# One product over three rows in place of two: the level updates of a gated scan

## The chip, the core and the metric

The kernel runs on one core of a Trainium2 chip. The metric is the device time of one execution in microseconds; a kernel's time is the median of its runs. TensorE (PE) multiplies matrices, VectorE (DVE) and ScalarE (ACT) work on elements, GpSimd (POOL) does small things and issues some DMAs, SyncE (SP) issues the others. Each engine has its own instruction stream and takes it in order; semaphores tie the streams together.

## The reference

One step of a decoder layer: RMS norm, a projection of 2048 prompt tokens and 8 decode tokens from 1024 to 8 × 512 columns, two groups of four heads of width 128, a head norm, a SiLU gate, the output projection, the residual and a final norm. The first four heads are retention with a fixed decay; the other four, HGRN2, have a decay of their own for each token and key column, and the change lies in these:

```
logf = logaddexp(log(lb), log1p(-lb) + log_sigmoid(hf))     # f = lb + (1 - lb) sigmoid(hf)
kin  = (1 - lb) * sigmoid(-hf)
q    = silu(hq)
S_t  = diag(f_t) S_{t-1} + k_t v_t^T,   o_t = S_t^T q_t       # computed in chunks
```

Inside a chunk the scores are A[t, s] = sum over d of q[t, d] k[s, d] times the product of f[., d] from s+1 to t. It is this product of decays that the levels build up.

## The kernel before, in words

Before about 570 us the kernel makes the projections of values, gates and the retention group, and runs the retention heads. Then come the HGRN2 heads, eight **units**: four heads for the first 1024 tokens, then the same four for the second 1024. A unit's keys and queries lie as [128 key columns, 1024 tokens] and its chunks have 128 tokens. At the end stands the output projection (lines 1648 to 1899).

The work on a unit is spread over three iterations. In the first, PE makes its f and q projections (matmuls of line 1039), each as three products of high and low parts. ACT turns them into f (line 1088) and k (line 1089), DVE into q and qt = q f (lines 1096 and 1098). In the second iteration the scan's **levels** run (`hgrn_rec`). In the third comes the **rest** (`tail_steps`, line 1106): the states (lines 1126 to 1134), the outputs (lines 1142 and 1144; the latter reads qt), their squares on ACT (line 1148), a reciprocal root on POOL (lines 111 and 112), the gated norm on DVE (line 1157), a transpose on PE (line 1164), an ACT copy (line 1166) and a store. So three units are in work at a time: while one is projected, the one before is scanned, and the one before that is finished.

The levels have block sizes b = 1, 2, 4, ... 64 (line 31). At each, small PE matmuls make the scores between the left and the right half of every block of 2b tokens, and then k of the left halves is multiplied by the decay over the right half, and qt of the right halves by the decay over the left half. That is `update` (lines 1220 to 1230): two DVE products of 512 columns each, lines 1225 (k) and 1228 (qt). The decays of all blocks come from `products` (line 1216). A unit has seven updates.

Three times in a unit (levels 1, 3 and 5) `keep` (line 1232) copies k and the right halves of qt to a buffer with two ACT instructions (lines 1235, 1236) before it updates them. The kept copy feeds the matmuls of one level (line 1255, or 1300 at level 5), the updated tiles those of the next (line 1255, or 1305 at level 6). So a pair of matmul groups can run while the next update is being made. `put` (line 1261) merges a level's scores on DVE under a mask.

What sets the order: PE's instructions stand as the program writes them. `merge` puts the steps of the levels and of the rest among the projection matmuls at written fractions of the iteration (the lists at the end of `hgrn_rec`). The order on the other engines is made by the framework's scheduler from its own estimates, except where `behind` (line 124) puts a step behind the last instruction issued on DVE, ACT and SP. Buffers come from pools: f, k and the pair q, qt have two buffers each, so a new unit's tile can be written when the tile of two units before is no longer read. Other work shares DVE and ACT in these iterations: the splits of weights and inputs into high and low parts (lines 115, 116), the output weights' sums (lines 1358 to 1364), and the decode tokens (lines 855 to 874).

Of the kernel before, what the change touches and what calls it, by code (L numbers as in the profile page):

```python
# [10 lines left out]
F32 = mybir.dt.float32  # L11
# [3 lines left out]
ALU = mybir.AluOpType  # L15
# [3 lines left out]
P = 128  # L19
# [3 lines left out]
HALF = T // 2  # L23
NB = 8
# [17 lines left out]
def step_kernel(ctx, tc, a, out):  # L42
    nc = tc.nc
    pe, act, dve, pool, sp = nc.tensor, nc.scalar, nc.vector, nc.gpsimd, nc.sync
# [960 lines left out]
    pools = {}  # L1005
# [48 lines left out]
    def sub_steps(half, j, name, evac, seg_list=None):  # L1054
        box = []

        def w():
            if not box:
                box.append(w_next(j))
            return box[0]  # L1060

        return [seg_steps(w, half, seg, name, evac) for seg in SEGS[half]]
# [6 lines left out]
    def hgrn_proj(half, h):  # L1069
        name = f"h{half}{h}"  # L1070
        u = {}

        def alloc():
            if not u:
                for x, b in (("f", 2), ("k", 2)):
                    u[x] = pools["ep"].tile([P, HALF + NB], F32, tag=f"u{x}", name=f"{x}{name}", bufs=b)
                u["qq"] = pools["ep"].tile([P, 2, HALF + NB], F32, tag="uqq", name=f"qq{name}", bufs=2)
                u["q"], u["qt"] = u["qq"][:, 0], u["qq"][:, 1, :HALF]
            return u

        def evac_f(t0, n, ps):
            f, k = alloc()["f"], u["k"]
            tt = slice(t0, t0 + n)
            xr = pools["tp"].tile([P, 512], F32, tag="tmp", name=f"fx{name}{t0}")
            sg = pools["tp"].tile([P, 512], F32, tag="tmp", name=f"fs{name}{t0}")
            act.activation(sg[:, :n], ps, AF.Sigmoid)
            act.activation(xr[:, :n], ps, AF.Sigmoid, scale=-1.0)
            act.activation(f[:, tt], sg[:, :n], AF.Identity, scale=lb1[:, h : h + 1], bias=lb[:, h : h + 1])
            act.activation(k[:, tt], xr[:, :n], AF.Copy, scale=lb1[:, h : h + 1])

        def evac_q(t0, n, ps):
            f, q, qt = (alloc()[x] for x in ("f", "q", "qt"))
            tt = slice(t0, t0 + n)
            sg = pools["tp"].tile([P, 512], F32, tag="tmp", name=f"qs{name}{t0}")
            act.activation(sg[:, :n], ps, AF.Sigmoid)
            dve.tensor_tensor(q[:, tt], ps, sg[:, :n], op=ALU.mult)
            m = min(t0 + n, HALF)
            dve.tensor_tensor(qt[:, t0:m], q[:, t0:m], f[:, t0:m], op=ALU.mult)

        steps = [  # L1100
            sub_steps(half, HF * NH + h, "f" + name, evac_f),
            sub_steps(half, HQ * NH + h, "q" + name, evac_q),
        ]
        return u, steps
# [83 lines left out]
    def hgrn_rec(half, h, u):  # L1188
        name = f"h{half}{h}"
        hd = NH + h  # L1190
        f, k, q, qt = u["f"], u["k"], u["q"], u["qt"]
# [8 lines left out]
        def views(b):  # L1200
            return (
                qt.rearrange("p (n two b) -> p n two b", two=2, b=b),
                k[:, :HALF].rearrange("p (n two b) -> p n two b", two=2, b=b),
            )

        def spans(li):
            if li == 0:
                return f[:, :HALF]
            at = HALF - (HALF >> (li - 1))
            return box["fp"][:, at : at + (HALF >> li)]  # L1210
# [8 lines left out]

        def update(li):  # L1220
            b = LEVELS[li]
            qv, kv = views(b)
            nb = HALF // (2 * b)
            two = spans(li).rearrange("p (n two) -> p n two", two=2)
            dve.tensor_tensor(  # L1225
                kv[:, :, 0, :], kv[:, :, 0, :], two[:, :, 1:2].to_broadcast([P, nb, b]), op=ALU.mult
            )
            dve.tensor_tensor(  # L1228
                qv[:, :, 1, :], qv[:, :, 1, :], two[:, :, 0:1].to_broadcast([P, nb, b]), op=ALU.mult
            )  # L1230

        def keep(li):
            b = LEVELS[li]
            ss = pools["ep"].tile([P, 3 * 512], F32, tag="kept", name=f"kept{name}{li}")
            act.activation(ss[:, 512:], k[:, :HALF], AF.Copy)  # L1235
            act.activation(
                ss[:, :512].rearrange("p (n b) -> p n b", b=b), views(b)[0][:, :, 1, :], AF.Copy
            )
            box["kept"] = ss
            update(li)  # L1240
# [26 lines left out]
        def scores0():  # L1267
            box["Ab"] = pools["up"].tile([P, CH, 32], F32, tag="Ab", name=f"Ab{name}")
            pa = ps_lv.tile([P, CH, 2, 32], F32, tag="lv", name=f"pa{name}")
            for c in range(CH):  # L1270
                for i in range(4):
                    cc = slice(c * P + 32 * i, c * P + 32 * i + 32)
                    pe.matmul(pa[32 * i : 32 * i + 32, c], k[:, cc], u["qq"][:, :, cc], start=True, stop=True)
            update(0)
            dve.tensor_tensor(
                box["Ab"], pa[:, :, 0], id32.unsqueeze(1).to_broadcast([P, CH, 32]), op=ALU.mult
            )
            put(pa[:, :, 1].rearrange("p c (n two b) -> p c n two b", two=2, b=1)[:, :, :, 1, :], 0)
            keep(1)

        def level(li, n):
            b = LEVELS[li + n]
            if n == 0:
                box["pl"] = ps_lv.tile([P, 2, CH, 16], F32, tag="lv", name=f"pl{name}{li}")
                small(box["pl"][:, 0], li, box["kept"])
            else:
                small(box["pl"][:, 1], li + 1)
                update(li + 1)
            put(box["pl"][:, n].rearrange("p c (n b) -> p c n b", b=b), li + n)
            if n:  # L1290
                keep(li + 2)
# [185 lines left out]
    def unit(i):  # L1477
        half, h = order[i]
        u, subs = hgrn_proj(half, h)
        steps = []  # L1480
        if i in SEG_MAJOR:
            for n in range(len(SEGS[half])):
                group = []
                for sub in subs:
                    group += sub[n]
                if (i, n) in sides:
                    group = weave(group, sides[i, n](), 0.0, 1.0 if i not in (3, 7) or (i, n) == (3, 1) else 0.6)
                steps += group
        else:
            for sub in subs:  # L1490
                for g in sub:
                    steps += g
        return steps, u
# [73 lines left out]
    for i in range(len(order)):  # L1567
        fill, u = unit(i)
# [297 lines left out]
    op = ctx.enter_context(tc.tile_pool(name="op", bufs=1))  # L1866
# [117 lines left out]
```

## Time and profile before

| | |
|---|---|
| runs | 1041.09, 1041.21, 1044.4 us; median 1041.21 |
| the profiled execution's span | 1040.8 us |
| busy: PE, DVE, ACT, POOL | 1028.0, 746.6, 554.1, 125.8 us |
| products of line 1225 / 1228 | 56 each; 0.69 / 0.68 us |
| ACT copies of lines 1235 / 1236 | 24 each; 1.06 / 0.64 us |
| place of the updates in the span | 605 to 886 us |

A row of a timeline is: start, duration, engine, line, operation, the written tile, the read tiles, the shape, and in brackets how long the engine stood idle before it and what released it. A row of a group has the count behind x, the busy time in all and the mean, then the idle time before. In a row of busy time by stretch the figures stand in the order PE, PE's weight loads, DVE, ACT, POOL, granted clock, share of the DMA engines, GB/s. Names in tiles: `kh` is k, `qqh` the pair q and qt, `fh` the decays, `fph` their products, `kepth` the kept copy, `plh` and `pah` the scores' banks, `poh` the outputs, `obh` the normed outputs, `poth` their transposes.

### The profile page before, as it was taken

Reading aid. Unit: us, or ns where it says so; the run is one execution under the profiler, and the core shown is the slowest. Engines: PE = TensorE matmul, PEld = TensorE weight load, DVE = VectorE, ACT = ScalarE, POOL = GpSimd, SP = SyncE. Lnnn points to the kernel's source line nnn. Section 1 sums busy time; section 2 is a strip of 40 time slices with the busy share of each in tenths; the row PEclk is TensorE's granted clock in tenths of the full one; section 3 lists DMA queues with packets and bytes.
Section 4 is the critical chain, followed back from the end, with each engine's and each line's share of the span. In section 5 each row is a group of like instructions: output and inputs, shape, how many; then the busy total and the mean of one; then the engine's idle time right before and its main releaser. Section 6 shows DMA issues by size and latency. Waiting matters only on the chain.

```text
span 1040.8 us, 21338 instructions
## 1 busy us (share of the span) xinstructions
PE 1028.0 (99%) x8231; PEld 851.5 (82%) x8231; DVE 746.6 (72%) x1387; ACT 554.1 (53%) x1209; POOL 125.8 (12%) x231
## 2 busy tenths in 40 slices
PE   9999999999999999999999999999999999999997
PEld 7778778787778888888888889898878888888775
DVE  6886676888665876666665767868767676667886
ACT  7853345635435765545554756565555465533242
POOL 0210001000000111111111100111022112312122
PEclk9999999999999999999999999999999999999999
DMA  8689999679998975487775696754785195575652
GB/s 298 214 325 336 321 335 310 266 252 318 312 333 301 366 248 161 163 274 218 231 255 165 244 321 212 259 161 161 236 255 189 36 382 206 161 286 187 240 183 102
DMA packets 151270, 255.61 MB, mean 246 GB/s; under 512 B 11424, under 2 KB 79280, under 8 KB 151040
## 3 DMA queue, kind: packets, MB, share of 16 engines
q1 hardware_dynamic: 143584, 229.22, 65.2%
q0 software_dynamic: 7440, 24.76, 6.2%
q8 instruction: 65, 1.06, 0.4%
q14 instruction: 37, 0.30, 0.1%
q10 hardware_dynamic: 144, 0.26, 0.1%
HBM read 166.51 MB, written 87.69 MB: 244 GB/s over the span
## 4 chain that ended last, share of the span: by engine, by line
PE 87%; DMA 6%; ACT 3%; DVE 2%; issue 1%; SPq 1%; POOL 0%; POOLq 0%; ACTq 0%; DVEq 0%
PE po L360 11%; PE pjqh L1039 9%; PE pjfh L1039 9%; PE py L1662 4%; PE plh L1255 2%; DMA xn<-in_x_prompt 2%; PE poh L1142 1%; PE par L744 1%; PE puh L1126 1%; PE pur L751 1%; PE por L757 1%; DMA T3l<-ws1T 1%; PE poh L1144 1%; PE por L759 1%; PE pv20a L360 1%
## 5 line engine op out<-in xcount | busy, mean ns | idle before, releaser
L1039 PE MATMUL pjfh<-xh,w_h 128*128 128x512 f32 (+2 forms) x160 | 59.9, 375 | 0.0
L1039 PE MATMUL pjqh<-xh,w_h 128*128 128x512 f32 (+2 forms) x160 | 59.8, 374 | 0.0
L1235 ACT ACTIVATE kepth<-kh 128x1024 f32<-128x1024 f32 x24 | 25.4, 1060 | 62.8 <-DVE kh L1225 62.7
L1039 PE MATMUL pjqh<-xh,w_l 128*128 128x512 f32 (+2 forms) x160 | 55.8, 349 | 0.0
L1039 PE MATMUL pjfh<-xl,w_h 128*128 128x512 f32 (+2 forms) x160 | 55.7, 348 | 0.0
L1039 PE MATMUL pjfh<-xh,w_l 128*128 128x512 f32 (+2 forms) x160 | 55.7, 348 | 0.0
L1039 PE MATMUL pjqh<-xl,w_h 128*128 128x512 f32 (+2 forms) x160 | 55.7, 348 | 0.0
L1225 DVE TENSOR_TENSOR kh<-kh,fph 128x512 f32<-128x512 f32 x48 | 33.4, 696 | 25.2 <-PE plh L1255 15.0
L116 DVE TENSOR_TENSOR ab_l<-xr,ab_h 128x512 fp32r<-128x512 f32 (+1 forms) x40 | 37.3, 954 | 6.6 <-ACT ab_h L115 6.6
L782 DVE SCALAR_TENSOR_TENSOR obr<-por,omr,rg 128x128 f32<-128x128 f32 x64 | 18.0, 345 | 32.3 <-POOL omr L774 27.6
L115 ACT ACTIVATE ab_h<-xr 128x512 fp32r<-128x512 f32 (+1 forms) x40 | 32.4, 840 | 15.2 <-DVE xr L313 15.2
L772 ACT ACTIVATE obr<-por 128x128 f32<-128x128 f32 x64 | 16.8, 277 | 43.4 <-PE por L759 41.1
L419 ACT ACTIVATE vo<-vo 128x512 f32<-128x512 f32 x32 | 20.1, 629 | 27.3 <-DVE vo L413 13.7
L1039 PEld LDWEIGHTS pjqh<-xh,w_h 128*128 128x128 f32 x160 | 30.2, 188 | 5.1 <-issue 1.6
L1039 PEld LDWEIGHTS pjqh<-xh,w_l 128*128 128x128 f32 x160 | 30.1, 188 | 4.1
L1039 PEld LDWEIGHTS pjfh<-xh,w_l 128*128 128x128 f32 x160 | 30.1, 188 | 4.1
L1039 PEld LDWEIGHTS pjfh<-xh,w_h 128*128 128x128 f32 x160 | 30.2, 189 | 3.8
L1228 DVE TENSOR_TENSOR qqh<-qqh,fph 128x512 f32<-128x512 f32 x48 | 32.8, 683 | 0.0
L313 DVE SCALAR_TENSOR_TENSOR xr<-xr,g_in,rb 128x256 f32<-128x256 f32 x64 | 27.0, 480 | 7.8 <-issue 5.0
L1039 PEld LDWEIGHTS pjqh<-xl,w_h 128*128 128x128 f32 x160 | 30.2, 189 | 2.7
L1039 PEld LDWEIGHTS pjfh<-xl,w_h 128*128 128x128 f32 x160 | 30.3, 189 | 2.7
L1157 DVE SCALAR_TENSOR_TENSOR obh<-poh,orsh,v 128x128 f32<-128x128 f32 x64 | 18.0, 344 | 13.4 <-POOL orsh L112 13.4
(1840 smaller groups left out, 3385.6 us busy)
## 6 DMA issues: line engine op xcount, KB each, us to landing
xr<-a_dram SPq DMA_DIRECT2D x24, 512.0 KB, 5.5
S<-s_dram SPq DMA_DIRECT2D x24, 512.0 KB, 5.6
xn<-in_x_prompt SPq DMA_DIRECT2D x32, 256.0 KB, 3.6
xr<-in_x_t SPq DMA_DIRECT2D x16, 512.0 KB, 6.1
a_dram<-xr SPq DMA_DIRECT2D x16, 512.0 KB, 4.1
s_dram<-S SPq DMA_DIRECT2D x16, 512.0 KB
wgr<-in_w SPq DMA_DIRECT2D x16, 512.0 KB, 8.7
xr<-a_dram SPq DMA_DIRECT2D x32, 256.0 KB, 4.4
```

What stands on the lines that cost most here:

```text
L115: act.activation(h, src, AF.Copy)
L116: dve.tensor_tensor(l, src, h.bitcast(F32), op=ALU.subtract)
L313: dve.scalar_tensor_tensor(r[:, k], r[:, k], g_in[:, kk : kk + 1], spread_to[i], op0=ALU.mult, op1=ALU.mult)
L360: pe.matmul(ps, xx, ww, start=(first and n == 0), stop=(last and n == 2), skip_group_check=more)
L419: act.activation(o, src, AF.Silu)
L782: dve.scalar_tensor_tensor(o[:, cc], po[:, h], ms[:, h : h + 1], rb_of[c, "g"][:, cc], op0=ALU.mult, op1=ALU.mult)
L1039: pe.matmul(ps, ww[:, kk], x[:, k, b0 : b0 + n], start=(k == 0 and i == 0), stop=(k == KT - 1 and i == 2),)
L1225: dve.tensor_tensor(kv[:, :, 0, :], kv[:, :, 0, :], two[:, :, 1:2].to_broadcast([P, nb, b]), op=ALU.mult)
L1228: dve.tensor_tensor(qv[:, :, 1, :], qv[:, :, 1, :], two[:, :, 0:1].to_broadcast([P, nb, b]), op=ALU.mult)
L1235: act.activation(ss[:, 512:], k[:, :HALF], AF.Copy)
L1255: pe.matmul(dst[32 * i : 32 * i + 32, c], kk, qq, start=True, stop=True)
L1662: pe.matmul(ps, o[:, kk], w[:, k % 4, i * 512 : (i + 1) * 512], start=(k == 0 and n == 0), stop=(k == KT - 1 and n == 2),)
```

## The change

The tile k and the tile with the two rows q and qt become one tile `qk` with the rows q, qt, k, with two buffers as before. `update` becomes one DVE product of 1024 columns: its operand has a dimension of two, row qt from column b on and row k from column 0 on, which lie row − b columns apart; its other operand is the span of decays, left one for qt and right one for k. The number of columns multiplied is the same. Line numbers behind the place are lower by 4 in the kernel after.

```diff
         def alloc():
             if not u:
-                for x, b in (("f", 2), ("k", 2)):
-                    u[x] = pools["ep"].tile([P, HALF + NB], F32, tag=f"u{x}", name=f"{x}{name}", bufs=b)
-                u["qq"] = pools["ep"].tile([P, 2, HALF + NB], F32, tag="uqq", name=f"qq{name}", bufs=2)
-                u["q"], u["qt"] = u["qq"][:, 0], u["qq"][:, 1, :HALF]
+                u["f"] = pools["ep"].tile([P, HALF + NB], F32, tag="uf", name=f"f{name}", bufs=2)
+                u["qk"] = pools["ep"].tile([P, 3, HALF + NB], F32, tag="uqk", name=f"qk{name}", bufs=2)
+                u["qq"] = u["qk"][:, 0:2]
+                u["q"], u["qt"], u["k"] = u["qk"][:, 0], u["qk"][:, 1, :HALF], u["qk"][:, 2]
             return u
...
         def update(li):
             b = LEVELS[li]
-            qv, kv = views(b)
-            nb = HALF // (2 * b)
-            two = spans(li).rearrange("p (n two) -> p n two", two=2)
-            dve.tensor_tensor(
-                kv[:, :, 0, :], kv[:, :, 0, :], two[:, :, 1:2].to_broadcast([P, nb, b]), op=ALU.mult
-            )
-            dve.tensor_tensor(
-                qv[:, :, 1, :], qv[:, :, 1, :], two[:, :, 0:1].to_broadcast([P, nb, b]), op=ALU.mult
-            )
+            nb, row = HALF // (2 * b), HALF + NB
+            x = u["qk"][:, 1]
+            both = bass.AP(x.tensor, x.offset + b, [list(x.ap[0]), [row - b, 2], [2 * b, nb], [1, b]])
+            two = spans(li).rearrange("p (n two) -> p two n", two=2)
+            dve.tensor_tensor(both, both, two.unsqueeze(3).to_broadcast([P, 2, nb, b]), op=ALU.mult)
```

PE's and POOL's instructions keep their order. On DVE and ACT the scheduler makes a new one. Three places follow.

DVE, the first two updates of the first unit's scan, before:

```order
609 L1225 TENSOR_TENSOR kh_5675<-kh_5675,fh_5674 128x512
610 L1228 TENSOR_TENSOR qqh_5676<-qqh_5676,fh_5674 128x512
611 L1275 TENSOR_TENSOR Abh_5861<-pah_5862,pk 128x256
612 L1261 COPY_PREDICATED Abh_5861<-lmask,pah_5862 128x128
613 L1225 TENSOR_TENSOR kh_5675<-kh_5675,fph_5836 128x256x2
614 L1228 TENSOR_TENSOR qqh_5676<-qqh_5676,fph_5836 128x256x2
```

and in the kernel after:

```order
609 L1226 TENSOR_TENSOR qkh_5675<-qkh_5675,fh_5674 128x2x512
610 L1271 TENSOR_TENSOR Abh_5860<-pah_5861,pk 128x256
611 L1257 COPY_PREDICATED Abh_5860<-lmask,pah_5861 128x128
612 L1226 TENSOR_TENSOR qkh_5675<-qkh_5675,fph_5835 128x2x256x2
613 L1257 COPY_PREDICATED Abh_5860<-lmask,plh_5934 128x64x2
```

Each pair of rows has become one row; nothing else moved here.

ACT, where the second unit is scanned, the third projected and the first finished, before:

```order
520 L1088 ACTIVATE fh_6408<-fsh_6486,lb,lb_168 128x256
521 L1089 ACTIVATE kh_6409<-fxh_6485,lb_168 128x256
522 L1235 ACTIVATE kepth_6533<-kh_5923 128x1024
523 L1236 ACTIVATE kepth_6533<-qqh_5924 128x512
...
527 L1148 ACTIVATE jkh_6572,omsh_6565<-poh_6557 128x128
528 L1086 ACTIVATE fsh_6611<-pjfh_768_6491 128x264
529 L1087 ACTIVATE fxh_6610<-pjfh_768_6491 128x264
530 L1088 ACTIVATE fh_6408<-fsh_6611,lb,lb_168 128x264
531 L1089 ACTIVATE kh_6409<-fxh_6610,lb_168 128x264
532 L1148 ACTIVATE jkh_6599,omsh_6598<-poh_6589 128x128
533 L1148 ACTIVATE jkh_6601,omsh_6598<-poh_6589 128x128
```

and after:

```order
519 L1088 ACTIVATE fh_6397<-fsh_6474,lb,lb_168 128x256
520 L1231 ACTIVATE kepth_6520<-qkh_5920 128x1024
521 L1232 ACTIVATE kepth_6520<-qkh_5920 128x512
...
525 L1148 ACTIVATE jkh_6558,omsh_6551<-poh_6543 128x128
526 L1086 ACTIVATE fsh_6597<-pjfh_768_6479 128x264
527 L1087 ACTIVATE fxh_6596<-pjfh_768_6479 128x264
528 L1088 ACTIVATE fh_6397<-fsh_6597,lb,lb_168 128x264
529 L1089 ACTIVATE qkh_6398<-fxh_6399,lb_168 128x512
530 L1089 ACTIVATE qkh_6398<-fxh_6473,lb_168 128x256
531 L1148 ACTIVATE jkh_6585,omsh_6584<-poh_6575 128x128
532 L1089 ACTIVATE qkh_6398<-fxh_6596,lb_168 128x264
533 L1148 ACTIVATE jkh_6587,omsh_6584<-poh_6575 128x128
```

The three evacuations of k (line 1089) stood behind their own f; two of them have moved behind the first four squares (line 1148) and one in between the second four. In the later iterations one or two of them move in the same way.

DVE, the fourth unit's scan (the fifth is projected, the third finished), before:

```order
767 L116 TENSOR_TENSOR xl_7451<-xr_7581,xh_7450 128x1024
768 L1225 TENSOR_TENSOR kh_6971<-kh_6971,fph_7440 128x128x4
769 L1228 TENSOR_TENSOR qqh_6972<-qqh_6972,fph_7440 128x128x4
...
773 L1358 TENSOR_TENSOR wot_7611<-wot_7610,wot_7609 128x512
774 L1096 TENSOR_TENSOR qqh_7586<-pjqh_0_7593,qsh_7734 128x512
775 L116 TENSOR_TENSOR xl_7451<-xr_7616,xh_7450 128x1024
776 L1360 TENSOR_TENSOR wot_7609<-wot_7609 128x512
777 L1098 TENSOR_TENSOR qqh_7586<-qqh_7586,fh_7584 128x512
778 L1362 TENSOR_TENSOR wot_7611<-wot_7610,wot_7609 128x512
779 L1157 SCALAR_TENSOR_TENSOR obh_7746<-poh_7683,orsh_7700,v_7089 128x128 x4
```

and after:

```order
747 L1226 TENSOR_TENSOR qkh_6952<-qkh_6952,fph_7415 128x2x128x4
...
750 L1354 TENSOR_TENSOR wot_7583<-wot_7582,wot_7581 128x512
751 L1096 TENSOR_TENSOR qkh_7558<-pjqh_0_7565,qsh_7704 128x512
752 L116 TENSOR_TENSOR xl_7426<-xr_7588,xh_7425 128x1024
753 L1356 TENSOR_TENSOR wot_7581<-wot_7581 128x512
754 L116 TENSOR_TENSOR xl_7426<-xr_7554,xh_7425 128x1024
755 L1098 TENSOR_TENSOR qkh_7558<-qkh_7558,fh_7557 128x512
756 L1358 TENSOR_TENSOR wot_7583<-wot_7582,wot_7581 128x512
757 L1157 SCALAR_TENSOR_TENSOR obh_7716<-poh_7653,orsh_7670,v_7067 128x128 x4
```

One subtraction of 1024 columns (line 116) has moved from ahead of the update with b = 4 to between line 1096 and line 1157, where now two of them stand.

## The prediction

> **What bounds the kernel now.** I read the page's head first, then busy time by stretch for the part in which the change works, then the waits of TensorE (PE), then the rows around the moved instructions.
>
> ```profile
> span 1040.8 us, 21338 instructions
> PE 1028.0 (99%) x8231; PEld 851.5 (82%) x8231; DVE 746.6 (72%) x1387; ACT 554.1 (53%) x1209; POOL 125.8 (12%) x231
> ...
> PE 87%; DMA 6%; ACT 3%; DVE 2%; issue 1%; SPq 1%; POOL 0%; POOLq 0%; ACTq 0%; DVEq 0%
> ...
> L1225 DVE TENSOR_TENSOR kh<-kh,fph x48: 681/693/727, 607.6 to 885.0; 128x512 f32<-128x512 f32 x48
> ...
> 600.00:650.00 50.00, 50.00 (x836) 44.73 (x836) 36.78 (x81) 30.20 (x61) 0.20 (x2) 1.00 0.77 267
> ...
> sum 300.00, PE 300.00 PEld 253.64 DVE 217.78 ACT 172.95 POOL 38.70; mean PE 50.00 PEld 42.27 DVE 36.30 ACT 28.83 POOL 6.45
> ```
>
> PE is the bound, and the chain that ended last runs mostly through it. The updates run from about 605 to 886 us; in the six stretches of 50 us from 600 to 900 PE is busy for all 300.00 us, and the granted clock is 1.00 in the first of them (the column after POOL). VectorE (DVE) is busy for 217.78 of these 300 us, ScalarE (ACT) for 172.95. Busy PE need not be PE at its peak, so I looked at the list of its waits and at the pitch of its long matmuls (start, duration):
>
> ```profile
> PE pgd L600 <- DMA wgr<-in_w: 1.2, 2, 0.7
> ...
> 725.38 0.39 PE L1039 MATMUL pjfh<-xl,w_h 128*128 128x512 f32 x1
> ...
> 727.68 0.39 PE L1039 MATMUL pjfh<-xh,w_l 128*128 128x512 f32 x1
> 727.91 0.60 PE L1164 MATMUL poth<-ident,obh 128*128 128x128 f32 x4
> ```
>
> From 725.38 to 727.68 there are ten steps in 2.30 us, 0.23 each, and the next kind of work follows at the same step: no gap. The first entry of the list of waits, its largest, is 1.2 us in 2 waits at line 600, and no line of the scan is on it. So the scan has no PE stall that a faster DVE could remove; it can only get new ones.
>
> **The change part by part.**
>
> *The multiplications.* There are 7 levels for each of 8 units: 56 pairs become 56 single instructions. Their prices:
>
> ```profile
> L1225 DVE TENSOR_TENSOR kh<-kh,fph 128x512 f32<-128x512 f32 x48 | 33.4, 696 | 25.2 <-PE plh L1255 15.0
> L1228 DVE TENSOR_TENSOR qqh<-qqh,fph 128x512 f32<-128x512 f32 x48 | 32.8, 683 | 0.0
> ...
> L116 DVE TENSOR_TENSOR xl<-xr,xh 128x1024 fp32r<-128x1024 f32 x8 | 9.8, 1221 | 1.6 <-ACT xh L115 1.6
> ```
>
> The trace has no such product over 1024 columns with a broadcast operand. The nearest row is the subtraction of 1024 columns, 1.22 us, which is also about the time that a pair holds DVE (below); the upper bound is 0.696 + 0.683 = 1.38. I take 1.22.
>
> ```profile
> 682.12 0.69 DVE L1225 TENSOR_TENSOR kh<-kh,fph 128x512 f32<-128x512 f32 x1 [1.95 <-PE plh L1255]
> 682.73 0.68 DVE L1228 TENSOR_TENSOR qqh<-qqh,fph 128x512 f32<-128x512 f32 x1
> 683.33 0.28 DVE L1261 COPY_PREDICATED Abh<-lmask,plh 128x128 f32<-128x128 uint8 x1
> 683.93 0.69 DVE L1225 TENSOR_TENSOR kh<-kh,fph 128x512 f32<-128x512 f32 x1 [0.32 <-ACT kepth L1235]
> 684.54 0.68 DVE L1228 TENSOR_TENSOR qqh<-qqh,fph 128x512 f32<-128x512 f32 x1
> ...
> 682.84 1.06 ACT L1235 ACTIVATE kepth<-kh 128x1024 f32<-128x1024 f32 x1 [4.90 <-DVE kh L1225]
> 683.81 0.62 ACT L1236 ACTIVATE kepth<-qqh 128x512 f32<-128x512 f32 x1
> ```
>
> The second product starts 0.61 us after the first, so successive instructions overlap by 0.08. The pair holds DVE from 682.12 to the next start at 683.33, 1.21 us; the merged one holds it about 1.22 − 0.08 = 1.14. That is 0.07 × 56, about 4 us of DVE, all of it beside 27% idle DVE and a full PE: worth 0 to the end.
>
> *What is later.* In a keep step both products run, ACT copies k and then q, and the next pair follows. Today ACT starts on k at 682.84, after the first product, while the second runs; and the next k product starts at 683.93, while q is still being copied. Merged, neither overlap is possible. From 682.12: the product ends at +1.22; the copies run 683.81 − 682.84 + 0.62 = 1.59 and end at about +2.84, where they now end at 684.43, +2.31: 0.53 later. The next product then runs from +2.87 to +4.09, where q now ends at 685.22, +3.10: **1.0 later**. There are three keep steps in a unit; the last is followed by the matmuls of line 1300, which need the copies, and of line 1305, which need the product. Line 1305 is thus the first place to stall. In the first unit:
>
> ```profile
> 624.25 0.69 DVE L1228 TENSOR_TENSOR qqh<-qqh,fph 128x512 f32<-128x512 f32 x1
> ...
> 626.04 1.14 PE L1305 MATMUL plh<-qqh,kh 128*64 128x64 f32 x16
> ```
>
> The product ends at 624.94 and is wanted at 626.04: 1.10 in hand, 1.0 used, 0 to 0.1 us of stall. The work that hides this second is PE's next projection matmuls; without them each unit would pay 1.0.
>
> *k's buffer.* k and the q rows now come free together, when the matmuls of line 1144 of two units earlier have read q. So the evacuations of k (line 1089) wait for PE, and stand behind or among the squares of line 1148, as the order shows for the stretch in which the second unit is scanned and the third is projected.
>
> ```profile
> 641.21 0.72 ACT L1089 ACTIVATE kh<-fxh,lb 128x512 f32<-128x512 f32 x1
> 645.15 0.51 ACT L1089 ACTIVATE kh<-fxh,lb 128x256 f32<-128x256 f32 x1
> 651.29 0.28 ACT L1148 ACTIVATE jkh<-poh 128x128 f32<-128x128 f32 x1 [0.21 <-PE poh L1144]
> 653.46 0.20 ACT L1148 ACTIVATION_READ_ACCUMULATOR jkh<-poh 128x1 f32 x1
> ...
> 653.75 0.57 POOL L111 TENSOR_SCALAR orsh<-omsh 128x4 f32<-128x4 f32 x1 [2.73 <-ACT jkh L1148]
> 654.39 1.53 POOL L112 TENSOR_TENSOR orsh<-orsh,mhalf 128x4 f32<-128x4 f32 x1
> 795.89 0.19 POOL L111 TENSOR_SCALAR orsh<-omsh 128x4 f32<-128x4 f32 x1 [5.95 <-ACT jkh L1148]
> 796.16 1.04 POOL L112 TENSOR_TENSOR orsh<-orsh,mhalf 128x4 f32<-128x4 f32 x1
> ...
> 655.96 1.13 DVE L1157 SCALAR_TENSOR_TENSOR obh<-poh,orsh,v 128x128 f32<-128x128 f32 x4 [0.90 <-POOL orsh L112]
> 657.36 0.69 DVE L1225 TENSOR_TENSOR kh<-kh,fph 128x512 f32<-128x512 f32 x1 [0.27 <-PE plh L1255]
> ...
> 658.75 0.60 PE L1164 MATMUL poth<-ident,obh 128*128 128x128 f32 x4
> 662.04 1.15 PE L1305 MATMUL plh<-qqh,kh 128*64 128x64 f32 x16
> ```
>
> The second group of squares ends at 653.66. It gets some 1.7 us later: 0.64 + 0.43 + 0.43 for three evacuations, one of 512 columns and two of about half (each holds ACT 0.08 less than its duration, as I take it from DVE), and some 0.2 because the first of them can begin only when PE is done, near 651.2. POOL's reciprocal root and line 1157 follow. POOL took 2.17 us there, 653.75 to 655.92, and 1.31 near 796; line 1157 would begin 1.7 later with the slow POOL, at 657.7, and 0.86 earlier than that with the quick one, at 656.8. The update now starts 1.40 behind it, 0.27 of that in a wait for PE that will be over: 1.13 is left, so it starts between 657.9 and 658.8. With the +4.09 from above its next product ends between 662.0 and 662.9, and line 1305 starts at 662.04 today: 0 to 0.9 of stall. I take **0.5**.
>
> *One subtraction moved.* In the fifth iteration (fourth unit's scan) one more 1024-column subtraction stands ahead of line 1157:
>
> ```profile
> 723.17 0.69 DVE L1096 TENSOR_TENSOR qqh<-pjqh,qsh 128x512 f32<-128x512 f32 x1 [1.27 <-PE poh L1144]
> 723.78 1.22 DVE L116 TENSOR_TENSOR xl<-xr,xh 128x1024 fp32r<-128x1024 f32 x1
> 724.91 0.69 DVE L1360 TENSOR_TENSOR wot<-wot 128x512 f32<-128x512 f32 x1
> ...
> 726.72 1.12 DVE L1157 SCALAR_TENSOR_TENSOR obh<-poh,orsh,v 128x128 f32<-128x128 f32 x4
> ```
>
> Line 1096 waits for PE, so the row of work behind it cannot move up. The subtraction holds DVE 724.91 − 723.78 = 1.13 us. Line 1157 now ends at 727.84, and its transposes start at 727.91 (quoted above): 0.07 in hand. They would start 1.1 later: **1.1** of stall, 0 if DVE finds a gap that the order does not show.
>
> *The others.* The third and the four later units have more in hand or the same order as the first; I give them 0.4 together, between 0 and 2 for all six units that are not named. The sum is 0.5 + 1.1 + 0.4 = 2.0 us, with bounds of 0 and 0.9 + 1.1 + 2 = 4.0. On the profiled 1040.8 us this is 1042.8; the median of the runs stands 0.4 above the span, so 1043.2.
>
> **A rule weighed.** POOL's two small instructions of the reciprocal root do not always take the same time:
>
> ```profile
> 798.50 1.24 POOL L111 TENSOR_SCALAR orsh<-omsh 128x4 f32<-128x4 f32 x1 [1.30 <-ACT jkh L1148]
> ...
> 798.47 1.22 DVE L855 TENSOR_TENSOR dv<-dv,dk 128x1024 f32<-128x1024 f32 x1
> ```
>
> It began with a 1024-column product on DVE and lasted until that ended, 1.05 us longer than the one at 795.89. A merged product can do the same where a short one would have held POOL for at most 0.69; the difference, 0.5 us, lies within the bounds of the second unit. The Trainium skill, "SBUF — State Buffer", section "SBUF: two separate sides", states this against the change: a DVE operation with two SBUF inputs holds the port pair that it shares with GpSimd for its whole length, and the other blocks. This row agrees; by the rule the second unit would pay its upper bound, and the sum would be 2.4 instead of 2.0.
>
> **The rivals.**
>
> *Slower: the merged product is too long a block.* The 1.0 us lag is paid in full if one more long instruction of DVE slips between the copies and the next product. Its place is the last keep step, the price the 1.13 us of one subtraction. With the numbers above the first unit, with 0.1 left in hand, would pay 1.0 more and the second 1.1; half of that is taken for the third and the fourth, 0.55 each, and nothing for the later ones: 3.2 in addition, 1046.4. It decides as soon as more than 1.10 us is lost ahead of line 1305. For it: DVE's order is made anew, and puts the subtractions elsewhere. Against: the order as built shows none in that place. Chance 0.24.
>
> *Faster: PE is paced by DVE after all.* Busy PE would hide short waits, and the relief of DVE would return: at most 4 us, 1037. Against it stands the even pitch of 0.23. Chance 0.06. The Trainium skill, "Perfetto Trace Analysis", section "Identifying the Most-Contended Engine", speaks for it: matmul busy time is a poor measure, and the share of weight loads is to be used, which here is 253.64 of 300, 85%; by that rule PE has room that DVE's saving could use.
>
> *Slower by much: the three-row operand runs below one column a step.* If the merged instruction took twice the pair, 2.4 us, every keep step would be longer by 2 × 1.2, and after 1 to 3 us in hand each of eight units would stall about 1.5: 1055. Against it: line 1225 has 681 to 727 ns over all spans from 2 to 64, so small runs of columns cost nothing. Chance 0.02.
>
> **How the numbers follow.** The forecast, 1043.2 with its own range of 1041.2 to 1045.2, has 0.68. Less than 0.3% (3.1 us) can't be told from no change; that is 1038.1 to 1044.3. Of the forecast 0.06 lies above 1044.3, of the first rival 0.18 of its 0.24, with 0.02 for the last: slower 0.26. Faster needs more than 3.1 of the 4 us that the relief can give: 0.05. Same 0.69. The range runs from 1040.4 (no stall, and 0.8 of DVE's relief returned) to 1047.0 (the first rival and 0.6 more).
>
> **What would show it.** Right: merged products of 1.20 to 1.25 us; ACT's k copy starting 0.5 later behind its product; DVE's busy time lower by 5 to 9 us; PE waits of about 1.1 us ahead of the transposes near 728, and of 0.5 ahead of line 1305 near 662; nothing after 900 us changed. Wrong: PE's scan without new waits and the time below 1041; stalls in most units; or a merged product above 1.4 us.

## The result and the profile after

Twenty runs of each kernel: 1043.81 us after (median; 1041.6 to 1046.09) and 1041.43 us before (1038.78 to 1044.4). The ratio is **1.0019, 95% interval 1.0012 to 1.0026**: by it 2.0 us slower (the medians differ by 2.4), less than 0.3% and yet clear of zero. Forecast were 1043.2 and 2.0 us. All ratios here are of fast runs; in the experiments four executions of 1271 to 3600 us (one of `free_and_pinned`, two of `three_moved`, one of the kernel before) are left out of them.

The head of the page of the kernel after, with the groups of the merged product and of the k copy:

```profile
span 1040.5 us, 21296 instructions
PE 1028.1 (99%) x8231; PEld 851.0 (82%) x8231; DVE 741.9 (71%) x1331; ACT 552.8 (53%) x1209; POOL 125.3 (12%) x231
...
L1226 DVE TENSOR_TENSOR qkh<-qkh,fph 128x1024 f32<-128x1024 f32 x48 | 58.7, 1223 | 38.8 <-ACT kepth L1232 21.4
L1231 ACT ACTIVATE kepth<-qkh 128x1024 f32<-128x1024 f32 x24 | 25.4, 1060 | 73.3 <-DVE qkh L1226 73.3
```

Two of its stretches of 50 us, and the sum of all six (columns as in the first part):

```profile
700.00:750.00 50.00, 49.65 (x718) 40.49 (x717) 38.34 (x78) 29.62 (x61) 4.28 (x6) 1.00 0.60 201
850.00:900.00 50.00, 49.18 (x598) 40.74 (x597) 34.77 (x62) 25.25 (x54) 8.56 (x17) 1.00 0.58 200
sum 300.00, PE 298.84 PEld 251.49 DVE 211.24 ACT 169.96 POOL 39.14; mean PE 49.81 PEld 41.91 DVE 35.21 ACT 28.33 POOL 6.52
```

All waits of PE between 590 and 930 us (total, count, longest):

```profile
PE py L1658 <- DVE wol L1530: 0.8, 1, 0.8
PE plh L1301 <- DVE qkh L1226: 0.3, 1, 0.3
```

DVE has 56 instructions fewer and is busy for 4.7 us less. PE, which was busy for all 300.00 us from 600 to 900, is now busy for 298.84: 1.1 us of it is the two waits on the list. More is lost than the list shows, because PE's weight loads (PEld) wait too. So I compare the start of the same PE instructions. Here are the first scores of the first unit (`pah`), and the level-6 scores of the third, fourth and eighth unit, before:

```profile
604.50 1.15 PE L1273 MATMUL pah<-qqh,kh 128*32 128x64 f32 x64
...
698.01 1.15 PE L1305 MATMUL plh<-qqh,kh 128*64 128x64 f32 x16
734.52 1.14 PE L1305 MATMUL plh<-qqh,kh 128*64 128x64 f32 x16
883.54 1.15 PE L1305 MATMUL plh<-qqh,kh 128*64 128x64 f32 x16
```

and after:

```profile
602.31 1.15 PE L1269 MATMUL pah<-qkh 128*32 128x64 f32 x64
...
695.73 1.15 PE L1301 MATMUL plh<-qkh 128*64 128x64 f32 x16
733.51 1.12 PE L1301 MATMUL plh<-qkh 128*64 128x64 f32 x16 [0.26 <-DVE qkh L1226]
883.37 1.15 PE L1301 MATMUL plh<-qkh 128*64 128x64 f32 x16
```

This one execution came to the scan 2.2 us earlier than the profiled one of before. Such an offset differs from profile to profile: two profiles of one kernel below (`tile_two_products` and `tile_two_again`) have −1.2 and 0.0, and `free_copy`, which differs from the kernel after in the scan alone, has +0.7. So it isn't the change's; it is also why the span is no longer than before although the runs are slower. Counted from the first scores, the **drift** of PE is −0.1 us at the third unit (698.01 − 604.50 = 93.51 against 93.42), +1.2 at the fourth, and +2.0 at the eighth. The scan loses 2.0 us, and it loses them in two places: 1.3 around 727 to 734, and 0.8 at 858. Behind 900 us the drift falls to 1.8, since a wait of 0.2 us that the profile before has at 927 is missing in the one after.

The second place was already tight before the change. The list of PE's waits before shows nothing there, but the weight loads waited for the same low part of the output weights, and the matmul on it started 0.38 us behind the one ahead (857.86) where the pitch is 0.23:

```profile
858.24 0.19 PEld L1662 LDWEIGHTS py<-wol,oc_h 128*128 128x128 f32 x1 [0.42 <-DVE wol L1534]
```

So the kernel before had nothing in hand at this place, and lost about 0.3 us in it.

**The first place.** DVE, ACT and PE's weight loads in the fourth unit's scan after:

```profile
720.81 0.69 DVE L1096 TENSOR_TENSOR qkh<-pjqh,qsh 128x512 f32<-128x512 f32 x1 [0.29 <-PE poh L1144]
723.34 1.22 DVE L116 TENSOR_TENSOR xl<-xr,xh 128x1024 fp32r<-128x1024 f32 x1
725.67 1.12 DVE L1157 SCALAR_TENSOR_TENSOR obh<-poh,orsh,v 128x128 f32<-128x128 f32 x4
...
721.46 0.71 ACT L1089 ACTIVATE qkh<-fxh,lb 128x512 f32<-128x512 f32 x1
722.07 1.05 ACT L115 ACTIVATE xh<-xr 128x1024 fp32r<-128x1024 f32 x1
...
724.61 0.19 PEld L1039 LDWEIGHTS pjfh<-xl,w_h 128*128 128x128 f32 x1 [0.47 <-DVE xl L116]
726.08 0.91 PEld L1164 LDWEIGHTS poth<-ident,obh 128*128 128x128 f32 x4 [0.48 <-DVE obh L1157]
```

and the two ACT rows as they stood before:

```profile
713.67 0.72 ACT L1089 ACTIVATE kh<-fxh,lb 128x512 f32<-128x512 f32 x1
714.29 1.05 ACT L115 ACTIVATE xh<-xr 128x1024 fp32r<-128x1024 f32 x1
```

The moved subtraction (line 116, 723.34) delays the normed blocks of line 1157, as forecast, and the transposes wait. It is also late for its own reader: the f projection waits for the low part. In PE's starts the f projection loses 0.3 us, the start of the transposes another 0.2, and the four transposes, each of which waits for its own normed block, 0.5. And the subtraction did not move by chance. The split (ACT copy of line 115, then this subtraction) is issued `behind` the last ACT instruction, and that is the evacuation of k, line 1089, at 713.67 before. After the change this evacuation waits for the joint tile and runs at 721.46, behind squares of line 1148 and another copy; so the copy that stood at 714.29 runs at 722.07.

**The keep steps.** Two products of the fourth unit with the copies between them:

```profile
715.82 1.23 DVE L1226 TENSOR_TENSOR qkh<-qkh,fph 128x1024 f32<-128x1024 f32 x1 [1.54 <-PE plh L1251]
717.08 1.06 ACT L1231 ACTIVATE kepth<-qkh 128x1024 f32<-128x1024 f32 x1 [5.16 <-DVE qkh L1226]
718.05 0.61 ACT L1232 ACTIVATE kepth<-qkh 128x512 f32<-128x512 f32 x1
718.69 1.22 DVE L1226 TENSOR_TENSOR qkh<-qkh,fph 128x1024 f32<-128x1024 f32 x1 [1.44 <-ACT kepth L1232]
```

The copies end at +2.84, the second product starts at +2.87 and ends at +4.09: to the hundredth what the prediction worked out from the rows of before. In 13 of the 16 keep steps of levels 3 and 5 the second product ends at +4.08 to +4.10; in the other three (fourth, fifth and eighth unit) other work stands in between.

### The profile page after: what moved, and what is told of

It reads as the page before. It is cut to its first block, busy times and chain, and to the rows that moved or that the text cites. A ratio compares the mean times of both kernels' runs of the same rounds, so it can differ in the third digit from the quotient of the medians.

```text
span 1040.5 us, 21296 instructions
## 1 busy us (share of the span) xinstructions
PE 1028.1 (99%) x8231; PEld 851.0 (82%) x8231; DVE 741.9 (71%) x1331; ACT 552.8 (53%) x1209; POOL 125.3 (12%) x231
## 4 chain that ended last, share of the span: by engine, by line
PE 91%; DMA 4%; ACT 2%; DVE 2%; issue 1%; SPq 0%; POOLq 0%; POOL 0%; ACTq 0%
PE po L360 11%; PE pjqh L1039 9%; PE pjfh L1039 9%; PE py L1658 4%; PE plh L1251 2%; DMA xn<-in_x_prompt 2%; PE poh L1142 1%; PE par L744 1%; PE puh L1126 1%; PE pur L751 1%; PE por L757 1%; PE por L759 1%; PE poh L1144 1%; PE pv20a L360 1%; PE pv21a L360 1%; PE pv22a L360 1%
## 5 line engine op out<-in xcount | busy, mean ns | idle before, releaser
L1226 DVE TENSOR_TENSOR qkh<-qkh,fph 128x1024 f32<-128x1024 f32 x48 | 58.7, 1223 | 38.8 <-ACT kepth L1232 21.4
L1231 ACT ACTIVATE kepth<-qkh 128x1024 f32<-128x1024 f32 x24 | 25.4, 1060 | 73.3 <-DVE qkh L1226 73.3
L1658 PE MATMUL py<-woh,oc_h 128*128 128x512 f32 x64 | 26.8, 419 | 0.0
```

The source lines that it names most:

```text
L1226: dve.tensor_tensor(both, both, two.unsqueeze(3).to_broadcast([P, 2, nb, b]), op=ALU.mult)
L1658: pe.matmul(ps, o[:, kk], w[:, k % 4, i * 512 : (i + 1) * 512], start=(k == 0 and n == 0), stop=(k == KT - 1 and n == 2),)
```

## The experiments

The figures of drift are those of PE's starts, counted as above from the first scores of the first unit; ratios are to the kernel before on the same chip.

| run | tile, products | drift at unit 3, 4, 8 | ratio (95%) |
|---|---|---|---|
| after | one tile, merged | −0.1, 1.2, 2.0 | 1.0019 (1.0012 to 1.0026) |
| after_again | the same | −0.1, 1.2, 2.0 | 1.0020 (1.0010 to 1.0029) |
| free_copy | merged, split untied | 0.0, 0.2, 1.1 | 1.0005 (0.9996 to 1.0014) |
| free_and_pinned | and an order of DVE | 0.0, 0.3, 1.0 | 1.0009 (1.0000 to 1.0018) |
| tile_two_products | one tile, two products | 0.0, 0.8, 1.6 | 1.0010 (1.0001 to 1.0019) |
| tile_two_again | the same | −0.1, 0.7, 0.9 | one run |
| tile_free_two | the same, split untied | −0.1, −0.2, −0.2 | one run |
| kept_by_two | mixed, split untied | 0.8, 0.7, 1.2 | 1.0010 (0.9996 to 1.0025) |
| three_moved | merged, three things moved | 0.0, 0.2, −0.1 | 0.9999 (0.9984 to 1.0015) |
| last_product_twice | merged, level 5 doubled | 4.2, 6.8, 9.3 | one run |

**The split untied** (`free_copy`).

```diff
-    def behind(f):
+    def behind(f, free=()):
...
-            for i in last.values():
-                es.enter_context(tc.issue_after(i))
+            for e, i in last.items():
+                if e not in free:
+                    es.enter_context(tc.issue_after(i))
...
-            behind(lambda: x_split(blk, kp, raw[kp]))
+            behind(lambda: x_split(blk, kp, raw[kp]), (act.engine,) if (blk, kp) == (3, 2) else ())
```

> The kernel after, with one tie taken away: the split of the third part of the fourth token block (ACT copy of line 115, DVE subtraction of line 116) is no longer tied behind the last ACT instruction issued before it, which is the evacuation of k (line 1089) of the fifth unit. That moves exactly these two instructions back to their old places. Theory A (k's buffer is held by q, the evacuation waits for PE, and the split that is tied behind it comes late; PE then waits for the low part and for the normed blocks near 725): the stall of the fourth unit's scan goes, 1.0 us there and the 0.3 us at its level-6 scores; the scan costs PE 0.8 us more than before instead of 2.1, and the ratio to the kernel before is 1.0008. Theory B (the merged product is a long block that delays whatever stands behind it): nothing changes, 2.0 us more than before, ratio 1.0019.

In the order of DVE and of ACT one row each moved back, and nothing else. The waits of PE on the page of this run:

```profile
PE py L1659 <- DVE wol L1531: 0.8, 1, 0.8
PE plh L1302 <- DVE qkh L1227: 0.3, 1, 0.3
```

The 1.0 us near 727 is gone, and with it the two waits of the weight loads. The 0.3 us of the fourth unit's level-6 scores, which I had taken for a consequence, is still there, so the drift is 1.1 and not the 0.8 of theory A. Since only these two rows moved, it is the tie to k's evacuation that costs 1.0 us.

**An order of DVE for the eighth unit** (`free_and_pinned`). The state updates had moved ahead of the eighth unit's second product and of the low part of the output weights, for which PE waits at 858. This run puts them back, from the second one on.

```diff
+                    first = anchor.get("wol") if (name, g, j) == ("h12", 0, 1) else None
-                    dve.scalar_tensor_tensor(dst, src, decay(c), pu[:, j], op0=ALU.mult, op1=ALU.add)
+                    follow(first, lambda: dve.scalar_tensor_tensor(dst, src, decay(c), pu[:, j], op0=ALU.mult, op1=ALU.add))
```

> As the run before it, and in the eighth unit's scan the state updates of the seventh (line 1134) from the second one on are put behind the second low part of the output weights (line 1530), as they stood in the kernel before. Theory A (two places cost all of it): no new wait of PE is left between 593 and 900 us, PE's scan takes as long as before to within 0.2 us, ratio 1.0000 with DVE still 4 to 5 us less busy. Theory B (each keep step's lag of 1.0 us is paid by PE in several units, unseen): at least 1 us more than before, ratio 1.001 or above.

A miss: 0.7 of the 0.8 us is left. The drift of 1.0 and the ratio of 1.0009 come near the figures of theory B, but not by its picture: they stand in two waits, 0.3 and 0.7, and not in several units. The two products, ACT's copies, the high part (line 1541) and the low part (line 1543) of the output weights there:

```profile
851.17 1.23 DVE L1239 TENSOR_TENSOR qkh<-qkh,fh 128x1024 f32<-128x1024 f32 x1 [0.17 <-PE pah L1282]
854.14 1.23 DVE L1239 TENSOR_TENSOR qkh<-qkh,fph 128x1024 f32<-128x1024 f32 x1 [0.16 <-ACT kepth L1245]
855.28 1.22 DVE L1543 TENSOR_TENSOR wol<-wor,woh 128x1024 fp32r<-128x1024 f32 x1
...
853.46 0.65 ACT L1245 ACTIVATE kepth<-qkh 128x512 f32<-128x512 f32 x1
854.00 2.95 ACT L1541 ACTIVATE woh<-wor 128x1024 fp32r<-128x1024 f32 x3
...
856.55 0.50 PE L1672 MATMUL py<-wol,oc_h 128*128 128x512 f32 x1 [0.69 <-DVE wol L1543]
```

Whatever the order, the second product can't start before the q copy ends at 854.11, and the weights' high part stands behind that copy on ACT. So it is the lag of the keep step that reaches PE here, by way of the copy, the second product and the low part behind them. The same three starts before:

```profile
853.55 0.69 DVE L1225 TENSOR_TENSOR kh<-kh,fh 128x512 f32<-128x512 f32 x1 [0.40 <-PE pah L1273]
855.47 0.72 DVE L1225 TENSOR_TENSOR kh<-kh,fph 128x512 f32<-128x512 f32 x1
856.96 1.23 DVE L1534 TENSOR_TENSOR wol<-wor,woh 128x1024 fp32r<-128x1024 f32 x1
```

There the second pair starts 1.92 us behind the first, and the low part 3.41; here it is 2.97 and 4.11. The low part is later by 0.7, and that is the stall, since there was no room before.

**One tile, two products** (`tile_two_products`, `tile_two_again`). The merged call becomes two, with the tile left as it is:

```diff
-            dve.tensor_tensor(both, both, two.unsqueeze(3).to_broadcast([P, 2, nb, b]), op=ALU.mult)
+            wide = two.unsqueeze(3).to_broadcast([P, 2, nb, b])
+            for r in (1, 0):
+                dve.tensor_tensor(both[:, r], both[:, r], wide[:, r], op=ALU.mult)
```

> The one tile of three rows stays, but each update is two products of 512 columns again, k first. Theory A (the shared buffer is what costs in the fourth unit; the long product only costs by the order of the eighth): PE stalls by 1.0 us near 727 as in the kernel after, and nowhere else; the ratio is 1.0010. ACT's first kept copy follows the k product after 0.72 us again. Theory B (the long product costs): the scan takes PE as long as before, ratio 1.0000.

The shared tile alone brings 0.8 us near 727, all of it at the transposes; the level-6 scores and, in this run, the output weights then cost nothing. The other 0.8 us of the first of the two runs comes in one wait with no releaser:

```profile
726.98 1.10 PE L1164 MATMUL poth<-ident,obh 128*128 128x128 f32 x4 [0.19 <-DVE obh L1157]
...
765.38 0.39 PE L1039 MATMUL pjqh<-xl,w_h 128*128 128x512 f32 x1 [0.65 <-issue]
```

> The run tile_two_products once more, for a wait of 0.65 us on line 1039 near 765 that had no releaser in its profile. If it is chance, it is gone and 0.8 to 1.0 us of drift is left, all of it near 727; if it belongs to the kernel, it comes again and the drift is 1.6.

It did not come again: 0.7 us of drift at the fourth unit and 0.9 at the eighth, with waits of 0.19 at the transposes and, this time, 0.17 at the output weights. What the wait near 765 was stays open.

**The same with the split untied** (`tile_free_two`): the two edits above together.

> One tile of three rows, two products in each update, and the split of the fourth token block freed from k's evacuation. If the shared buffer costs only through that tie, nothing is left of the stall near 727 and PE's starts in the scan drift by less than 0.2 us against the kernel before. If the later evacuations of k cost elsewhere too, 0.5 us or more is left.

Nothing is left: the drift is −0.2 us and the list of PE's waits is empty in the scan. In this one run the shared tile costs through that tie only.

**Two products ahead of a copy, one elsewhere** (`kept_by_two`).

```diff
+            if li not in (0, 2, 4):
+                return dve.tensor_tensor(both, both, wide, op=ALU.mult)
+            for r in (1, 0):
+                dve.tensor_tensor(both[:, r], both[:, r], wide[:, r], op=ALU.mult)
```

> The split freed as in free_copy; the updates ahead of a kept copy (levels 0, 2 and 4) are two products again, k first, the other four are merged. Theory A' (it is the keep step's lag that meets PE at the level-6 scores of the fourth unit and at the output weights of the eighth): ACT starts its copy of k 0.7 us behind the k product instead of 1.25, the copies end as in the kernel before, the product behind them 0.5 us later than before instead of 1.0; both stalls fall below 0.2 us and PE's drift in the scan is 0 to 0.3 us, ratio 1.0001. If the merged product itself is at fault wherever it stands, the stalls stay at 0.3 and 0.8.

Half a miss. The fourth unit's stall is gone and that at the output weights is halved, but the first unit has a new one:

```profile
623.50 0.69 DVE L1097 TENSOR_TENSOR qkh<-pjqh,qsh 128x512 f32<-128x512 f32 x1 [0.68 <-ACT qsh L1096]
624.97 1.22 DVE L1229 TENSOR_TENSOR qkh<-qkh,fph 128x1024 f32<-128x1024 f32 x1
...
622.87 0.60 ACT L1096 ACTIVATE qsh<-pjqh 128x512 f32<-128x512 f32 x1 [4.69 <-PE pjqh L1040]
...
626.34 1.12 PE L1306 MATMUL plh<-qkh 128*64 128x64 f32 x16 [0.65 <-DVE qkh L1229]
...
858.94 0.50 PE L1663 MATMUL py<-wol,oc_h 128*128 128x512 f32 x1 [0.43 <-DVE wol L1535]
```

The scheduler, with new estimates, put q's sigmoid (line 1096 here) ahead of the kept copies on ACT. The sigmoid had to wait for PE, so the k copy started at 623.36, 2.04 us behind the start of the k product (621.32) instead of the expected 0.7: 1.3 us on ACT, and the first unit has 1.1 in hand, of which the merged product behind the copies takes 0.5. The forecast of this run, a ratio of 1.0001, was missed by that (1.0010).

**Three things moved** (`three_moved`): the split untied, the second copy of line 1166 put behind the kept copies of the fourth unit, and the second high and low part of the output weights issued earlier:

```diff
-        *((0.02 + 0.04 * n, lambda s=s: behind(s)) for n, s in enumerate(wo1[2])),
+        *(((0.02, 0.03, 0.1, 0.14)[n], lambda s=s: behind(s)) for n, s in enumerate(wo1[2])),
...
-            act.activation(ot, pt.rearrange("p a b -> p (a b)"), AF.Copy, scale=ng[:, hd : hd + 1])
+            first = kept_by.get(("h03", 5)) if (name, g) == ("h02", 1) else None
+            follow(first, lambda: act.activation(ot, pt.rearrange("p a b -> p (a b)"), AF.Copy, scale=ng[:, hd : hd + 1]))
```

> The merged product in all updates, the split freed as in the run free_copy, and the two other stalls met at their places: the second ACT copy of line 1166 (third unit) is put behind the kept copies of level 5 of the fourth unit, and the second pair of high and low parts of the output weights (lines 1528 and 1530) is issued right behind the first, ahead of the eighth unit's first update. Theory A' (the cost lies in three places: the split tied behind k's evacuation 1.0, the level-6 scores of the fourth unit 0.3, the output weights of the eighth 0.8): no wait of PE is left in the scan, PE's starts drift by less than 0.2 us against the kernel before between 600 and 900, the ratio is 1.0000. If the lag of the keep steps costs unseen in other units too, at least 0.5 us of drift is left.

In the main as expected: merged products, a drift of −0.1 us at the eighth unit, ratio 0.9999. But the −0.1 is a sum of two small things. At the level-6 scores of the fourth unit 0.2 us is still lost: another ACT instruction (`fxh`, line 1099 here) came ahead of the kept copies in place of the copy that was moved, and PE starts 0.15 us behind the end of the product, as it does wherever it waits for one (0.14 in the kernel after). At the output weights 0.3 us is gained, because there the loss that the kernel before has at 858 is gone too. To 0.2 us the three places are the whole cost. The kernel doesn't beat the one before, though DVE is busy for 741.1 us instead of 746.6: PE, with a pitch of its own, takes no part of that.

**The kernel after once more** (`after_again`), on the chip of the two runs above it, `kept_by_two` and `three_moved`.

> The kernel after once more, on the chip of the two runs before it: waits of PE at the split and the normed blocks near 727 (1.0 us), the level-6 scores of the fourth unit (0.3) and the output weights of the eighth (0.8), 2.0 to 2.1 us of drift in the scan, ratio 1.0019.

It repeats: drift 2.0, ratio 1.0020, the same waits of 0.3 and 0.8 us.

**The product of level 5 twice** (`last_product_twice`).

```diff
+            for _ in range(2 if li == 5 else 1):
                 dve.tensor_tensor(both, both, two.unsqueeze(3).to_broadcast([P, 2, nb, b]), op=ALU.mult)
```

> The kernel after with the product of level 5 applied twice in each unit, so the scores of level 6 and what follows use a decay too much: this part of the computation is changed. It puts 1.14 us more between the kept copy and the scores of line 1301. By the room that the trace of the kernel after shows ahead of these matmuls (0.14, 0.21, 0.49, 0.14, 0.93, 1.87, 1.06 and 1.20 us for the eight units, of which 0.14 is there even where PE waits), PE stalls by 1.14, 1.07, 0.79, 1.14, 0.35, 0, 0.22 and 0.08 us: 4.8 us in all beyond the kernel after. If the room is larger than it looks because PE's work around can shift, under 2 us.

A miss in size: the drift is 9.3 us, 7.3 beyond the kernel after instead of 4.8. PE stalls at the level-6 scores by 1.71, 1.55, 0.81, 1.51 and 0.86 us in the first five units; the fourth's holds the 0.3 that the kernel after has there. In the first, second and fifth it is more than expected because something else got in between. In the first unit:

```profile
625.88 1.22 DVE L1227 TENSOR_TENSOR qkh<-qkh,fph 128x1024 f32<-128x1024 f32 x1 [0.31 <-ACT kepth L1233]
627.02 0.68 DVE L1096 TENSOR_TENSOR qkh<-pjqh,qsh 128x512 f32<-128x512 f32 x1
627.62 1.21 DVE L1227 TENSOR_TENSOR qkh<-qkh,fph 128x1024 f32<-128x1024 f32 x1
...
628.98 1.11 PE L1302 MATMUL plh<-qkh 128*64 128x64 f32 x16 [1.71 <-DVE qkh L1227]
```

Line 1096 slipped between the two products and added 0.60: 1.14 + 0.60 = 1.74, against 1.71 measured. The second unit has the same row there (1.74 less the 0.07 it has in hand, 1.55 measured), and so has the fifth (0.95, 0.86 measured); the third has not (0.79, 0.81 measured). In these units the room ahead of the matmuls is what the trace shows it to be to 0.1 us, and a single row of 0.6 us decides. All waits at these matmuls make 6.7 us; less the 0.3 of the kernel after they leave 0.9 of the 7.3 that stands elsewhere, and its cause is open.

## Why the prediction was right, point by point

- **PE is the bound and has no stall to lose.** Right but for the 0.3 us at the output weights near 858, which stands in the weight loads and not on the list of waits that I went by. Where the new stalls are taken out (`three_moved`, `tile_free_two`) the scan is as long as before to within 0.2 us, whatever DVE is relieved of. The rival by which DVE's relief comes back is out, and with it what the Trainium skill's "Perfetto Trace Analysis", section "Identifying the Most-Contended Engine", would suggest here: weight loads busy for 85% were no room that could be used.
- **The merged product takes 1.22 us.** Right: 1.223. The steep rival (twice a pair) is out. DVE's busy time fell by 4.7 us, just under the 5 to 9 that I named for it among the signs, and near the 4 that the working gave.
- **The lag of 1.0 us in a keep step.** Right, to the hundredth in most steps. In the first unit the room ahead of line 1305 was to fall from 1.10 to 0.1; it fell to 0.14, and PE does not wait. ACT's k copy starts 1.26 us behind its product instead of 0.72, as named. But I let the lag end at the level-6 scores. It also reaches whatever stands behind the copies on ACT and behind the second product on DVE: the output weights of the eighth unit, 0.8 us. The term "the others", 0.4, should have been 0.8, and its reason was not seen. The statement that nothing changes after 900 holds to 0.2 us.
- **k's buffer and the second unit, 0.5.** It was 0, at the lower bound. Counted from the first scores the squares end 1.2 us later, not 1.7: the evacuations begin 0.1 ahead of where the squares began, not 0.2 behind, and the one between two squares costs 0.25, not 0.43. Line 1157 (654.42) starts only 0.6 later, because POOL's second instruction took 1.01 us instead of 1.53. The room there is nearly used up, without a stall:

```profile
658.33 1.23 DVE L1226 TENSOR_TENSOR qkh<-qkh,fph 128x1024 f32<-128x1024 f32 x1 [1.44 <-ACT kepth L1232]
...
659.77 1.15 PE L1301 MATMUL plh<-qkh 128*64 128x64 f32 x16
...
652.73 0.57 POOL L111 TENSOR_SCALAR orsh<-omsh 128x4 f32<-128x4 f32 x1 [3.57 <-ACT jkh L1148]
653.38 1.01 POOL L112 TENSOR_TENSOR orsh<-orsh,mhalf 128x4 f32<-128x4 f32 x1
```

  The second product ends at 659.56, 0.21 ahead of its reader. POOL's first instruction took 0.57 us beside a 1024-column subtraction, as the Trainium skill's "SBUF — State Buffer", section "SBUF: two separate sides", has it; the upper bound that I worked out by that rule was not reached all the same.
- **The moved subtraction, 1.1.** Right in size (1.0) and in place. Its 0.07 in hand set the end of the last normed block (727.84) against the start of the first transpose; the last transpose started at 728.23, so 0.39 was in hand. The reason given was too shallow. I took the move for the scheduler's and laid the price on the delay of line 1157; `free_copy` shows that the move hangs on k's evacuation, `tile_two_products` that it happens without any merged product, and the weight load at 724.61 that the f projection's own operand was late as well. The part on k's buffer, which I had costed at the second unit alone, was thus about half of the cost: 1.0 us for the tile, 1.1 (0.3 and 0.8) for the merged product.
- **The 0.3 us at the level-6 scores of the fourth unit.** Not in the sum. The second copy of line 1166 now stands ahead of the kept copies on ACT, since they come later:

```profile
729.96 0.68 ACT L1166 ACTIVATE oth<-poth,pk 128x512 f32<-128x512 f32 x1
730.53 1.06 ACT L1231 ACTIVATE kepth<-qkh 128x1024 f32<-128x1024 f32 x1
```

  Before, the product ended (733.69) 0.83 us ahead of its reader (734.52), and 0.14 of that is left even where PE waits. Now the copy ahead takes 0.57 of this room, and 0.46 goes because it is 2.84 us from the start of the kept copies (730.53) to the end of the product (733.37), where it was 2.38 (731.31 to 733.69). That is 0.3 too much.
- **The slow rival** (more long work between copies and product, 1046.4) did not come, but `kept_by_two` and `last_product_twice` show that its point of decision was rightly put: in the first unit one row of 0.6 us on DVE, or one on ACT that itself waits for PE, is paid by PE in that place.

So the main term was right, and the total was met in part by luck, with terms that missed in both directions: 0.5 (second unit) + 1.1 (fourth) + 0.4 (all others) was forecast, 0 + 1.3 + 0.8 measured, which is 2.0 with the 0.1 that the first three units gained.

## What to carry to other kernels

Merging two instructions of an engine that isn't the bound gained nothing here, and it delays the first consumer by the length of the second half: look for every reader that began on the first half, and follow the delay past that reader to what is queued behind it on its own engine. Putting two tensors in one tile ties their lifetimes together, so ask which write now waits for which last read, and what is ordered behind that write. Where the room ahead of the bound engine is 0.1 to 0.5 us, the scheduler's new order decides as much as the edit does; comparing the start of the same PE instructions in two traces finds each stall to 0.1 us, while the runs of one kernel spread over 4.5 to 5.6 us.

## What the runs showed that I had not expected

A wait of PE need not be on its own list of waits. Of the 1.0 us near 727 that list shows nothing: half of it stands behind two waits of the weight loads (0.47 and 0.48 us, of which PE's matmuls lose 0.3 and 0.2), and half in the four transposes, which took 1.10 us together instead of 0.60 since each waits for its own normed block. The same goes for the kernel before, which lost 0.3 us near 858 with nothing on the list. And in the scan one profile of eleven had a single gap of 0.65 us between two projection matmuls with no releaser, which did not come again when the same kernel was run once more.
